# A hybrid decoder layer on one NeuronCore: the attention's division moved behind its value products, and gate work cut into quarters

## The chip, the cores and the metric

The kernel runs on one core of a Trainium2 chip. The time is device microseconds of one execution of the whole program, inputs and weights read from HBM and the result written back. The kernel before was run three times outside the profiler; one more execution was profiled, and all rows below come from that one.

The engines are named as in the profile: PE is TensorE (PEld its weight loads), DVE is VectorE, ACT is ScalarE, POOL is GpSimd, SP issues nearly all DMAs. "SPq", "DVEq" and so on are the engines' instruction queues.

## What is computed

One decoder layer on x of 1024 tokens by 1024 channels, all in float32: a norm, one input projection, two mixers side by side, an output projection, a second norm and a gated MLP with a short convolution. The change touches the end of mixer A (its gated norm) and mixer B (the attention):

```python
z = z_a.astype(jnp.float32).reshape(B, S, GDN_HEADS, GDN_HEAD_DIM)
o_a = (rmsnorm(o_a, gdn_norm_w) * jax.nn.silu(z)).reshape(B, S, GDN_WIDTH).astype(x.dtype)
...
s = jnp.where(valid, s, -jnp.inf)
m = jnp.max(s, axis=-1)
p = jnp.exp(s - m[..., None])
den = jnp.sum(p, axis=-1)
num = jnp.einsum('...nqk,...nkd->...nqd', p, vv)
...
out = num_tot / den_tot[..., None]
...
x = x + jnp.concatenate([o_a, o_b], axis=-1) @ w_out
```

Mixer B has eight heads of 64 channels and three patterns of keys (near, every fourth, every sixteenth). The kernel joins the three patterns into one softmax per query, with the logarithm of each key's multiplicity in a mask.

## The kernel before

**Layout.** Activations lie transposed, channels on the 128 partitions and tokens along the free axis. Each float32 matrix product is three products of 128x128 by 128x512, of a high and a low part of each factor (`mm3`, L245). The low part is a subtraction on VectorE, the high part a rounding copy on ScalarE (`split`, L251).

**An order written out by a planner.** `Weave` (L46) runs several generators ("streams") with levels, keeps an estimate of TensorE's time and of when each tile is ready, and lets the most urgent stream that is ready emit its next products. The matmuls carry a token (`TOKEN`), so TensorE executes them in exactly this order and stands still if an operand is late. Instructions of the other engines are put in order by a scheduler with priorities; those written through `uv` and `ua` (L157, L158) go ahead of others. Work that can wait is cut into *pieces*: `defer` (L199) stores them, `background` (L226) emits one when the planner thinks VectorE is free, `flush` (L204) emits what must be there now. While attention or the recurrence runs (`chains` isn't empty), each piece is tied between the urgent operations around it.

**The streams around the change.** `dense` (L577) multiplies the normed input with 25 columns of 128 weights; the list `DENSE` (L42) ends with the attention's columns `("a", pair, part)` and the four `z` columns. Each column is two halves of 24 products. Its products fill TensorE while attention waits for the softmax. A column's weights come through the tag `wst` with two buffers.

`attention` (L1035) goes through four pairs of heads (`pi`), each in two halves of the queries (`hh`), so eight *groups*; a group has four query blocks `n`, handled in two pairs of blocks. Per pair `advance` (L1169) turns the probabilities of the pair before on TensorE (`turn`, L1112), makes the scores of this pair (`scores`, L1046), and multiplies the turned probabilities of the pair before with the values (`values`, L1131; after a group's last pair also `merge_classes`, L1140, for the far keys). `normalise` (L1078) is the softmax: minimum and mask on VectorE, exponential with its sum on ScalarE, then a reciprocal and two scalings on VectorE, in the tile `sm`. `turn` waits in the plan for `sm` of the pair's first block. A group's output lies in one PSUM bank `po` of the tag "ch" (two banks); `give` (L1154) copies it to `oT` in a reordered layout, and SP stores it in `mixer`.

`finish` (L984) sums the squares of mixer A's output and sends the sums through DRAM (`sdram`, `ft`) to POOL, which makes the norm's factor; `fdram` holds it. In `dense`, each z column loads the head's output `og` and the factor spread over all partitions, `fB` (`to_all`, L690), and POOL multiplies them (L636). `gate` (L552) makes tanh on ScalarE and two products on VectorE of 128x1024 each, `zz` and `og`; for the first three z columns it is put off behind a softmax (`put_off`). `scaled` (L507) evicts a z half from PSUM in one instruction.

After the dense columns, `mixer_splits` (L1217) splits the eight mixer tiles, `out_proj` (L1245) multiplies them with the output weights, first for two output blocks at once (j = 0 in banks "hf", j = 1 in banks "ch", the latter once attention is done), then block by block.

## Time and profile before

| What | Value |
|---|---|
| median of three runs | 1187.69 us (1185.7 to 1190.31) |
| the profiled execution's own time | 1187.61 us |
| its span in the profile | 1185.0 us, mean granted TensorE clock 0.998 |
| recurrence and dense columns, chains on | up to about 300 us |
| attention woven with dense columns | about 300 to 460 us |
| output projection | about 455 to 545 us |
| MLP | about 545 to 1185 us |

How to read the rows: in the timeline a row is the start in us, the duration in us (of all of a merged run), engine, line, operation, out<-in with partitions x elements, the count, and in brackets the idle time of that engine just before it with what ended it. L142, L144, L233 and L242 are lines of helpers through which nearly all instructions go: L142 plain, L144 urgent, L233 matmul, L242 half transposes of the probabilities. In group rows the numbers behind the bar are busy us of the whole group and mean ns of one; then idle time before them. Matmuls overlap: a 128x512 product's record is 0.39 us long while one starts every 0.23 us.

### The profile page before, as it was taken

How to read it: one execution, taken by the hardware profiler on the slowest of the kernel's cores; microseconds unless marked ns; L12 is line 12 of the kernel's file. 1: busy time of each engine (PE TensorE's matmuls, PEld its weight loads, DVE VectorE, ACT ScalarE, POOL GpSimd, SP SyncE). 2: the span in 40 equal slices, each digit the busy share in tenths (PEclk: the TensorE clock that was granted, in tenths of full speed). 3: DMA queues.
4: the chain of work that ended last, by engine and by line, in shares of the span. 5: the costliest groups of instructions: out<-in, count | busy, mean ns of one | idle time of the engine just before them, and what ended most of it. 6: DMA issues, size and time to landing. Idle time of an engine off the chain costs nothing.

```text
span 1185.0 us, 18118 instructions
## 1 busy us (share of the span) xinstructions
PE 1173.8 (99%) x6962; PEld 969.6 (82%) x6962; DVE 968.7 (82%) x1556; ACT 555.4 (47%) x996; POOL 65.8 (6%) x50
## 2 busy tenths in 40 slices
PE   9999999999999999999999999999999999999997
PEld 7888888898777778888888888888888888888887
DVE  7786997464687876768999898988889889998987
ACT  7483333333344444655554444544444543546452
POOL 0312001003130000000000000000000000000001
PEclk9999999999999999999999999999999999999999
DMA  7424566838563314443231313222231395456624
GB/s 240 108 88 138 149 162 181 263 103 250 192 187 100 87 51 150 164 139 107 89 107 54 107 54 107 72 88 93 68 107 54 132 386 184 127 177 223 239 96 160
DMA packets 120310, 165.34 MB, mean 140 GB/s; under 512 B 55008, under 2 KB 70176, under 8 KB 120224
## 3 DMA queue, kind: packets, MB, share of 16 engines
q1 hardware_dynamic: 119504, 163.66, 43.2%
q8 instruction: 54, 0.88, 0.3%
q10 hardware_dynamic: 720, 0.53, 0.1%
q14 instruction: 32, 0.26, 0.1%
HBM read 123.99 MB, written 40.17 MB: 139 GB/s over the span
## 4 chain that ended last, share of the span: by engine, by line
PE 96%; DVE 2%; SPq 1%; ACT 1%; DMA 0%; issue 0%; DVEq 0%; ACTq 0%
PE ps L233 46%; PE pa L233 20%; PE dw L233 18%; PE pc L233 10%; PE ps L242 1%; SPq L142 1%; DVE sm L144 1%; PE ps L237 1%; PE warm L233 0%; DMA wst<-in_wi 0%; DVE wlo L142 0%; DVE x1h L142 0%; ACT sm L144 0%; PE pd L233 0%; DVE pt L144 0%
## 5 line engine op out<-in xcount | busy, mean ns | idle before, releaser
L233 PE MATMUL dw<-pr 128*128 128x512 f32 (+1 forms) x984 | 211.4, 376 | 0.0
L233 PEld LDWEIGHTS dw<-pr 128*128 128x128 f32 x984 | 176.7, 188 | 33.6
L233 PE MATMUL ps<-xhi,whi 128*128 128x512 f32 x448 | 183.3, 409 | 0.0
L233 PE MATMUL ps<-xhi,wlo 128*128 128x512 f32 x448 | 175.2, 391 | 0.0
L233 PE MATMUL ps<-xlo,whi 128*128 128x512 f32 x448 | 175.0, 391 | 0.0
L233 PE MATMUL pa<-T,pair 128*128 128x512 f32 x528 | 126.8, 389 | 0.0
L233 PEld LDWEIGHTS pa<-T,pair 128*128 128x128 f32 x528 | 99.1, 188 | 20.6
L233 PEld LDWEIGHTS ps<-xhi,whi 128*128 128x128 f32 x448 | 84.5, 189 | 19.5 <-issue 3.1
L233 PEld LDWEIGHTS ps<-xhi,wlo 128*128 128x128 f32 x448 | 84.2, 188 | 18.4
L233 PEld LDWEIGHTS ps<-xlo,whi 128*128 128x128 f32 x448 | 84.6, 189 | 14.7
L142 ACT ACTIVATE u<-pa 128x512 f32<-128x512 f32 x44 | 26.4, 599 | 114.3 <-PE pa L233 114.3
L142 DVE SCALAR_TENSOR_TENSOR y<-xu,fcw,y 128x1023 f32<-128x1023 f32 (+1 forms) x44 | 56.3, 1281 | 22.1 <-ACT y L142 22.0
L142 ACT ACTIVATE pr<-wd 128x1024 fp32r<-128x1024 f32 x33 | 35.0, 1060 | 72.3 <-DVE wd L142 35.4
L142 DVE TENSOR_TENSOR wlo<-wst,whi 128x256 fp32r<-128x256 f32 (+3 forms) x65 | 50.9, 802 | 15.6 <-ACT whi L142 15.6
L233 PE MATMUL pa<-B,A 128*128 128x512 f32 x264 | 63.5, 389 | 0.0
L233 PE MATMUL pc<-T,S 128*128 128x512 f32 x264 | 63.4, 389 | 0.0
L233 PE MATMUL pc<-B,pair 128*128 128x512 f32 x264 | 63.4, 389 | 0.0
L233 PE MATMUL pa<-T,S 128*128 128x512 f32 x264 | 63.4, 389 | 0.0
L142 DVE TENSOR_TENSOR wst<-wst 128x512 f32<-128x512 f32 x88 | 60.4, 686 | 0.8
L233 PE MATMUL ps<-B,pair 128*128 128x512 f32 x252 | 60.5, 389 | 0.0
L144 ACT ACTIVATE sm<-sm,mx 128x128 f32<-128x128 f32 (+7 forms) x64 | 35.4, 555 | 51.6 <-DVE mx L144 51.6
L142 ACT ACTIVATE whi<-wst 128x1024 fp32r<-128x1024 f32 (+2 forms) x38 | 38.4, 1011 | 42.2 <-PE ps L233 28.4
(243 smaller groups left out, 2199.4 us busy)
## 6 DMA issues: line engine op xcount, KB each, us to landing
wst<-in_wu SPq DMA_DIRECT2D x44, 512.0 KB, 3.6
wd<-in_wd SPq DMA_DIRECT2D x44, 512.0 KB, 4.4
wst<-in_wi SPq DMA_DIRECT2D x25, 512.0 KB, 4.4
upark<-y SPq DMA_DIRECT2D x22, 512.0 KB, 3.4
r<-upark SPq DMA_DIRECT2D x22, 512.0 KB, 10.1
wa<-in_wd SPq DMA_DIRECT2D x22, 256.0 KB, 3.0
apark<-aqkv SPq DMA_DIRECT2D x8, 512.0 KB, 4.8
wst<-in_wo SPq DMA_DIRECT2D x8, 512.0 KB, 3.7
```

The source lines that it names most:

```text
L142: return getattr(eng, op)(*a, **kw)
L144: inst = getattr(eng, op)(*a, **kw)
L233: tc.stamp_issue_order_token(nc.tensor.matmul(dst, lhs, rhs, start=start, stop=stop, **kw).ins, TOKEN)
L237: tc.stamp_issue_order_token(nc.tensor.transpose(dst, src, ident).ins, TOKEN)
L242: tc.stamp_issue_order_token(nc.tensor.transpose(dst, src[rows], ident[rows, rows]).ins, TOKEN)
```

## The change

- The softmax's reciprocal and scaling of `sm` go; the probabilities stay undivided through turn, values and far keys.
- The sums go to a constant tile `dens` (eight columns for a group). After a group's last softmax `spread` takes the reciprocal of all eight columns, turns them (32x32 blocks) on VectorE, writes four pieces to DRAM (`dendram`) and loads them back so that each of the 64 partitions of a head holds the reciprocals of the 512 queries, in `rB`, a tile of the tag "uy" (five slots, of which four were in use in attention).
- `give` multiplies `po` with `rB`, in four instructions of 128x128, instead of copying. They wait in a list `lazy` until the load was emitted and no other piece is due; a list `soon` holds the spread's steps.
- `turn` waits in the plan for both blocks' `sm`, with other slacks (-0.1, -0.6 instead of -1.0 for the first block alone).
- The factor's product moves from POOL to VectorE, in quarters of 256 columns, and from the z columns to `finish`; a z column waits for ("g", h).
- z's eviction and the two gate products are issued in quarters through the piece list, tanh in halves; the `put_off` list goes.
- The first output weights are prepared while the last dense column runs, their subtractions in quarters; so are those of the third block. j = 1 starts once the last output is given. `background` runs on until all lists are empty.
- `sd` is SP's queue with another cost in the plan (0.4 + 0.0003 per element, 2.2 until landing); the loads of `vc` are booked by it as well.

```diff
@@ constants and lists
+    sd = Engine(wv, nc.sync, "sync", 0.4, 0.0003, 2.2)
-    pieces, chains, seen = [], set(), {}
+    pieces, lazy, soon, chains, seen = [], [], [], set(), {}
...
     def background():
-        while "attention" not in wv.done:
-            if pieces and wv.free.get("vector", 0.0) <= wv.pe + 0.05 and wv.need(*pieces[0][2]) <= 0.0:
-                one_piece()
+        while not {"attention", "firsts"} <= wv.done or pieces or lazy or soon:
+            while soon and wv.need(*soon[0][2]) <= 0.0:
+                one_piece(soon)
+            for queue in (pieces, lazy):
+                if (queue and wv.free.get("vector", 0.0) <= wv.pe + 0.05 and wv.need(*queue[0][2]) <= 0.0
+                        and all("spread" in g for g in queue[0][3:])):
+                    one_piece(queue)
+                    break
             yield 0.3
+        chains.discard("attention")
+        wv.done.add("drained")
...
+    dendram = dp.tile([2 * H, 8, P], F32, name="dendram")
+    dens = const("dens", [P, 4, 32])
+    ve.memset(dens, 1.0)
@@ gate
+    quarters = [slice(256 * i, 256 * i + 256) for i in range(4)]
+    def gate(og, xr, pt):
...
+            turned_on(slice(0, 512))
+            turned_on(slice(512, 1024))
+        defer(*[(y, lambda c=c: ve.scalar_tensor_tensor(y[:, c], y[:, c], 1.0, xr[:, c], op0=OP.add, op1=OP.mult), [y])
+                for c in quarters])
+        defer(*[(og, lambda c=c: product(c), [y, og]) for c in quarters])
@@ dense
             if kind == "z":
                 yield from wv.until(("o", h))
+                yield from wv.until(("g", h))
...
-            if i + 1 < len(DENSE):
+            if i + 1 == len(DENSE):
+                first_out.append(wk(I["wo"][MORDER[0]], None, 4))
+            else:
                 nxt = wk(None, raw.pop(), 4 if chains else 1)
...
+                if kind == "z":
+                    for c in quarters[2 * hh:2 * hh + 2]:
+                        defer((pt, lambda c=c, pt=pt, xr=xr: ve.tensor_tensor(xr[:, c], pt[:, c.start % 512:c.start % 512 + 256],
+                                                                              rstdB[:, c], op=OP.mult), [pt]))
...
-                to_all(fB[0], fdram[h])
-                po_.tensor_tensor(og, og, fB[0], op=OP.mult)
...
+                gate(gated[h], xr, pt)
@@ finish, behind "f"
+        fB = A("fB", "go")
+        for h in range(H):
+            og = gated[h] = A("og", "kT*")
+            sy.dma_start(og, mixer[h])
+            to_all(fB, fdram[h])
+            while wv.need(og, fB) > 0.0:
+                yield wv.need(og, fB)
+            defer(*[(og, lambda c=c, og=og: ve.tensor_tensor(og[:, c], og[:, c], fB[:, c], op=OP.mult),
+                     [og, fB]) for c in quarters])
+            while any(t is og for t, *_ in pieces):
+                yield 0.3
+            wv.done.add(("g", h))
@@ attention
-            uv.reciprocal(den, den)
-            for e in range(2):
-                div = uv.tensor_scalar(sm[:, e, :wd], sm[:, e, :wd], den[:, e:e + 1], None, op0=OP.mult)
+        def spread(g):
+            i = 2 * g["pi"] + g["hh"]
+            if not g["hh"]:
+                rBs.append(A("rB", "uy"))
+            rB = g["rB"] = rBs[-1][:, half(g["hh"])]
+            row, held = dens[:, 2 + i % 2], dendram[i]
+            def turn_():
+                ve.reciprocal(g["den"][:, :8], g["den"][:, :8])
+                inst = ve.transpose(row, g["den"])
+                for b in range(4):
+                    sd.dma_start(held[:, 32 * b:32 * b + 32], row[32 * b:32 * b + 8])
+                return inst
+            def load():
+                for e in range(2):
+                    r = held[4 * e:4 * e + 4]
+                    sd.dma_start(rB[64 * e:64 * e + 64],
+                                  bass.AP(tensor=r.tensor, offset=r.offset, ap=[[0, 64], [1, 4 * P]]))
+                g["spread"] = True
+            soon.append((g["po"], turn_, [g["den"]]))
+            soon.append((g["po"], load, [dendram]))
...
-                return max(wv.need(pair[0]["sm"]) + TSLACK[0], *[wv.slot_free(t, n) for t in ("asc", "atr")
+                return max(wv.need(pair[0]["sm"]) + (-0.1), wv.need(pair[1]["sm"]) + (-0.6), *[wv.slot_free(t, n) for t in ("asc", "atr")
...
-            ve.tensor_copy(oT.rearrange("p (n u c) -> p n c u", n=4, c=4),
-                           po.rearrange("p (n c u) -> p n c u", n=4, c=4))
+            def part_(n):
+                inst = ve.tensor_tensor(oT.rearrange("p (n u c) -> p n c u", n=4, c=4)[:, n],
+                                        po.rearrange("p (n c u) -> p n c u", n=4, c=4)[:, n],
+                                        g["rB"][:, n * P:n * P + P].rearrange("p (c u) -> p c u", c=4), op=OP.mult)
...
+            lazy.extend((po, lambda n=n: part_(n), [po, g["rB"]], g) for n in range(4))
...
+                if len(groups) > 1:
+                    flush(groups[-2], soon)
+                    flush(groups[-2], lazy)
                 po = bank("ch")
@@ out_proj
-        ws = [wk(I["wo"][m]) for m in MORDER[:2]]
+        made = first_out + [wk(I["wo"][MORDER[1]], None, 4)]
...
-            now = [a for a in todo if ("ot", a[0]) in wv.done and (a[1] == 0 or "attention" in wv.done)]
+            now = [a for a in todo if ("ot", a[0]) in wv.done and (a[1] == 0 or ("o", 7) in wv.done)]
```

101 lines of the change are left out of this document (53 added, 48 removed).

## The prediction

> **What bounds the kernel now.** I read the page first: span, busy shares, chain of waits.
>
> ```profile
> span 1185.0 us, 18118 instructions
> PE 1173.8 (99%) x6962; PEld 969.6 (82%) x6962; DVE 968.7 (82%) x1556; ACT 555.4 (47%) x996; POOL 65.8 (6%) x50
> ...
> PE 96%; DVE 2%; SPq 1%; ACT 1%; DMA 0%; issue 0%; DVEq 0%; ACTq 0%
> ```
>
> TensorE is the bound. The change adds and removes no matmul: the new turn of the reciprocals runs on VectorE, everything else is VectorE, ScalarE, POOL or DMA work. So it can pay only where TensorE stands still or changes its kind of work, and only in the stage it touches, attention woven with the dense columns, which the second view gives as one window (busy us of each engine, instructions in brackets).
>
> ```profile
> 300.00:460.00 160.00, 157.02 (x1723) 119.59 (x1722) 126.91 (x363) 67.62 (x208) 18.53 (x13) 1.00 0.40 120
> ```
>
> TensorE lacks 160 - 157.0 = 3.0 us there; VectorE is busy 79%. What follows is dense, from the chain of waits in order of time:
>
> ```profile
> 457.80 85.54 PE ps L233 x376
> ```
>
> That is 85.54/376 = 0.2275 us a product, with no gap to win. Third view: TensorE in order of time at every place of the stage where a bracket reports idle time.
>
> ```profile
> 335.64 0.71 PE L242 MATMUL ps<-ident,sm 64*128 64x64 f32 x16 [1.44 <-DVE sm L144]
> 336.55 0.73 PE L242 MATMUL ps<-ident,sm 64*128 64x64 f32 x16 [0.20 <-DVE sm L144]
> ...
> 397.45 2.39 PE L233 MATMUL ps<-kT,qT 64*128 64x256 f32 x40 [0.59 <-ACT pb L144]
> ...
> 405.57 0.50 PE L233 MATMUL ps<-xhi,whi 128*128 128x512 f32 x1
> ...
> 407.85 1.26 PE L233 MATMUL ps<-kT,qT 64*128 64x128 f32 x8
> ...
> 412.31 0.60 PE L242 MATMUL ps<-ident,sm 64*128 64x64 f32 x8 [0.57 <-DVE sm L144]
> ```
>
> The four brackets add to 1.44 + 0.20 + 0.59 + 0.57 = **2.80 us**. Three (2.21 us) wait for `sm`, the scaled softmax, the very tensor whose scaling goes. As ends of matmuls are modelled, some waiting hides inside long records; comparing runs of like products I put that at about 2 us more, an estimate. So about **5 us** is all that can be recovered as waiting, 0.4% of 1187.6.
>
> Why the largest wait was so long is seen on VectorE and POOL in order of time:
>
> ```profile
> 326.43 3.51 DVE L142 TENSOR_TENSOR wlo<-wst,whi 128x256 fp32r<-128x256 f32 x4
> ...
> 333.06 2.77 DVE L144 TENSOR_SCALAR sm<-sm,mx 128x416 f32<-128x416 f32 x2
> ...
> 401.92 0.78 DVE L144 TENSOR_SCALAR sm<-sm,mx 128x416 f32<-128x416 f32 x2
> ```
> ```profile
> 326.28 2.38 POOL L142 TENSOR_TENSOR og<-og,fB 128x1024 f32<-128x1024 f32 x1 [5.28 <-DMA fB<-fdram]
> ...
> 332.88 2.37 POOL L142 TENSOR_TENSOR og<-og,fB 128x1024 f32<-128x1024 f32 x1 [3.75 <-DMA fB<-fdram]
> ```
>
> The same two scalings take 0.78 us alone and 2.77 us while POOL multiplies `og`: 1.99 us lost, more than the 1.64 us for which TensorE then stood. The four subtractions beside the first POOL product took 3.51 us too; three alone take 1.08 (a row further down).
>
> **The change part by part.** VectorE's groups in the stage, with their shapes (busy us, mean ns):
>
> ```profile
> L142 DVE TENSOR_TENSOR wlo<-wst,whi 128x256 fp32r<-128x256 f32 x25 | 11.5, 499 | 0.0
> L142 DVE TENSOR_TENSOR aqkv<-ps,rstdB 128x256 f32<-128x256 f32 x16 | 9.1, 625 | 0.5 <-PE ps L233 0.5
> L142 DVE COPY oT<-ps 128x512 f32<-128x512 f32 x8 | 8.5, 1059 | 0.0
> L142 DVE TENSOR_TENSOR xr<-ps,rstdB 128x512 f32<-128x512 f32 x8 | 5.5, 689 | 1.5 <-PE ps L233 1.4
> L144 DVE RECIPROCAL mx<-mx 128x2 f32<-128x2 f32 x32 | 5.2, 164 | 3.1 <-ACT sm L144 2.5
> L142 DVE SCALAR_TENSOR_TENSOR og<-og,gw,zz 128x1024 f32<-128x1024 f32 x4 | 5.1, 1281 | 0.1
> L142 DVE SCALAR_TENSOR_TENSOR zz<-zz,xr 128x1024 f32<-128x1024 f32 x4 | 4.9, 1224 | 1.1 <-ACT zz L142 1.1
> L142 DVE STREAM_TRANSPOSE avt<-aqkv 128x256 f32<-128x256 f32 x8 | 3.0, 416 | 0.0
> L144 DVE COPY pt<-ps 128x128 f32<-128x128 f32 x8 | 1.9, 276 | 2.7 <-PE ps L242 2.7
> ```
> ```profile
> L144 DVE TENSOR_SCALAR sm<-sm,mx 128x128 f32<-128x128 f32 (+7 forms) x64 | 24.9, 431 | 1.2
> ```
>
> *Removed from VectorE*: the scalings 24.9, their reciprocals 5.2, the copies of `oT` 8.5, and, to be re-issued in quarters, z's evictions 5.5, `zz` 4.9, `og` 5.1: 54.1 us. *Added*: 32 multiplications of 128x128 out of PSUM, between the 0.28 us of a 128x128 copy and half a reordered 128x256 eviction and more (at most 0.63); I take 0.30, as half of 0.63 is 0.31: 9.6 us. Eight reciprocals of eight columns and eight turns of 128x32, each about 0.2 (the 0.16 of two columns below, the 0.42 of eight times the turn above): 3.2. Quarters for z, factor, sigmoid and gate, 16 each, at 0.42 (between 0.36, a third of 1.08 in the row quoted further down, and the group's 0.50): 64 x 0.42 = 26.9. Sum 39.7, so VectorE is relieved of 14 us; with the upper ends (20.2 + 6.7 + 32.0 = 58.9) it would gain 5 us of work. The low ends (9.0 + 2.6 + 23.0 = 34.6) give 20 us of relief. This is off TensorE's path except at the waits; I give it no value of its own.
>
> *The wait at 335.64* (1.64 us): turning then needs only the exponentials, no scaling, and POOL's product is gone from beside it: **-1.6**. *At 412.31* (0.57) the same: **-0.6**. *At 397.45* the wait is for `pb`, ScalarE's copy behind VectorE's `pt`, which stood behind a whole z eviction; a quarter is shorter by 0.69 - 0.42 = 0.27 us: **-0.3** of the 0.59. *Of the hidden 2 us* I take half, **-1.0**: the same chains feed them, but not all of it can be told from the cost of changing products. *Against it* **+0.5**: the added quarters must find their place between the urgent operations, and any one of them just ahead of a `pt` copy costs up to 0.42 us. Sum -1.6 - 0.6 - 0.3 - 1.0 + 0.5 = **-3.0 us**.
>
> *Spreading the reciprocals* is the new wait: four writes to DRAM, then two loads that wait for them, all on SP's queue, 48 issues in eight groups. The nearest row is the norm factor's own trip, written in four pieces and loaded back:
>
> ```profile
> 306.70 2.80 SPq L142 DMA_DIRECT2D sdram<-sums  x4
> ...
> 313.75 0.33 SPq L142 DMA_DIRECT2D ft<-sdram  x1
> ```
> ```profile
> 315.56 5.44 POOL L142 TENSOR_TENSOR ft<-ft,mhalf 128x32 f32<-128x32 f32 x1 [21.75 <-DMA ft<-sdram]
> ```
>
> 315.56 - 306.70 = 8.9 us. The kernel's planner, by the constants of the diff, books 4 x 0.41 + 2.2 + 2 x 0.55 + 2.2 = 7.1 us. The answer must be there before the output bank is due again, two groups on; the groups follow each other every (447.23 - 322.72)/7 = 17.8 us:
>
> ```profile
> 322.72 1.06 DVE L142 COPY oT<-ps 128x512 f32<-128x512 f32 x1
> ...
> 447.23 1.07 DVE L142 COPY oT<-ps 128x512 f32<-128x512 f32 x1
> ```
>
> So I cost it at nothing, covered by at least one group's matmuls. Without that cover a multiplication waits on VectorE for the load, and all urgent softmax work is queued behind it (rival below). The Trainium skill, "DMA: Bandwidth & Descriptors", section "Anatomy of one DMA — SWDGE (gpsimd) path", gives a fixed cost of about 2.0 us for a DMA, most of it the write receipt. Two in a row would make 4 us and the issues, well inside 7.1; the row's 8.9 us speaks for more, and I go by the row. Its specifications also put the least transfer at full rate at 512 bytes, which the 128-byte rows written here miss; no row shows what that costs.
>
> *The end of attention.* The last `oT` copy above ends at 448.3, and the first output product starts at 455.41:
>
> ```profile
> 455.41 0.39 PE L233 MATMUL ps<-ohi,whi 128*128 128x512 f32 x1
> ```
> ```profile
> 386.45 0.69 DVE L142 TENSOR_TENSOR xr<-ps,rstdB 128x512 f32<-128x512 f32 x1
> ...
> 439.04 0.17 DVE L144 RECIPROCAL mx<-mx 128x2 f32<-128x2 f32 x1 [0.30 <-ACT sm L144]
> ```
>
> The last reciprocal of now, which follows the last exponential, starts at 439.04, so 439.0 + 0.4 + 8.9 + 4 x 0.30 = 449.5, 1.2 us later than now, still 5.9 us before 455.41: hidden. The output weights' subtractions move earlier, in quarters, under the same dense products; `dens` costs one memset at the start. The factor's product moves from the z columns to right after `f`; its loads of `og` and `fB` keep their order on SP, the first two factors were there at 326.28 and 332.88 (above), four by that pace before 350, and z's first eviction comes at 386.45, so z need not wait for it. The other account for `vc` and the new slacks in `turn` change only the plan.
>
> **Rivals.** *One, slower: the reciprocals come late.* For three of the eight groups SP is then issuing the next heads' keys and values:
>
> ```profile
> 393.29 5.07 SPq L142 DMA_DIRECT2D vc<-avdram  x8
> ...
> 399.10 0.36 SPq L142 DMA_DIRECT2D wst<-in_wi  x1
> ```
> ```profile
> 388.66 1.08 DVE L142 TENSOR_TENSOR wlo<-wst,whi 128x256 fp32r<-128x256 f32 x3
> ```
>
> Eight issues hold the queue for 5.07 us, and a weight load behind them leaves only at 399.10. A spread behind these arrives after 8.9 + 5.1 = 14 us where 7.1 were booked in the worst case; VectorE in order then stands up to 6.9 us, of which a dense run (405.57 to 407.85, 2.28 us) covers about 2.3: 4.6 us on TensorE, three times 13.8; in the five other groups 8.9 - 7.1 = 1.8 us is covered. Two of the three in full and one by half make +11.5; less the 3.0: **1196.1**. It decides once the loads land over 2.3 us after the place where the planner put the multiplications. For it: SP is in order and its queue is full there. Against: the diff books `vc` dearer (0.55 an issue), and multiplications go out only when nothing else is waiting.
>
> *Two, no change:* VectorE was not the bound, the waits reappear at other points of a fixed TensorE order (`pb`, the quarters). Savings of 3.5 against new waits of 3.5: **1187.6**. For it: the bracket at 397.45 is not one of scaling.
>
> *Three, more:* every wait goes (-4.8), and the shorter softmax lets some of the changes between dense and attention products fall together. The nine dense products from 405.57 to 407.85 take 2.28 instead of 9 x 0.2275 = 2.05 us, so a change costs 0.23; eight fewer of some thirty: -1.8. **1181.0**. Against: the banks of scores still have to come free.
>
> **How the numbers follow.** The profiled execution took 1187.6 us (span 1185.0), as good as the median of 1187.69, so 1187.6 - 3.0 = **1184.6**. Chances: forecast 0.43, rival one 0.24, two 0.20, three 0.13. About 0.5%, or 5.9 us, is what a measurement of this kernel can tell from no change: below 1181.8 lies rival three, above 1193.6 rival one, hence faster 0.13, same 0.63, slower 0.24. The forecast's own range is 1182.5 to 1186.5 (savings of 5 us and 1 us); half of each outer rival is left out: 1181 to 1196, which also holds the unknown costs of the quarters.
>
> **What would show it.** Right: no `TENSOR_SCALAR` on `sm`, no POOL product of `og`, no bracket over 0.5 us on the turning matmuls; VectorE busy in this stage lower by 10 to 15 us. Wrong: a multiplication of `oT` whose idle time before it ends with the DMA of `rB`; matmuls waiting for `ps` behind it; weights (`whi`) waiting for `wst` behind the spread on SP. The out projection should start without a new gap. If TensorE's lack in this stage doesn't fall from 3.0 us, the reasoning fails.

## The result, and the profile after

| | before | after |
|---|---|---|
| median (9 runs each, same chip) | 1187.69 us (1185.7 to 1190.85) | **1184.32 us** (1183.52 to 1185.22) |
| ratio | 1 | 0.9971 (95%: 0.996 to 0.9983) |
| profiled execution, span in it | 1187.61, 1185.0 us | 1184.53, 1182.5 us |
| mean granted TensorE clock | 0.998 | 0.998 |

The changed kernel is 0.29% faster, 0.3 us from the forecast of 1184.6. With nine runs a side, the interval separates even this from no change, though the prediction took 0.5% as the least that can be told. The small net hides two larger movements, and the forecast had both wrong in size.

From the page of the changed kernel, the engines with busy time and share:

```profile
PE 1172.2 (99%) x6962; PEld 967.8 (82%) x6962; DVE 949.1 (80%) x1558; ACT 555.3 (47%) x1000; POOL 54.6 (5%) x46
```

TensorE's matmuls are the same 6962. VectorE has lost 968.7 - 949.1 = 19.6 us, the span only 2.5. Next the windows (length, then busy us of PE, PEld, DVE, ACT and POOL with instructions, granted clock, DMA share, GB/s): first of the kernel before, where its largest wait lay, then of the changed kernel for the same stretch and for the whole stage.

```profile
325.00:350.00 25.00, 23.36 (x274) 17.82 (x270) 23.29 (x65) 10.24 (x37) 10.79 (x7) 1.00 0.63 178
```
```profile
325.00:350.00 25.00, 24.95 (x275) 18.96 (x276) 16.16 (x59) 9.82 (x35) 0.84 (x2) 1.00 0.74 209
...
300.00:460.00 160.00, 158.08 (x1734) 120.49 (x1734) 107.65 (x365) 71.23 (x218) 9.00 (x9) 1.00 0.45 137
```

In the 25 us that held the wait at 335.64, VectorE drops from 23.3 to 16.2 us and POOL from 10.8 to 0.8, and TensorE stands for 0.05 instead of 1.64 us. Over 160 us TensorE still lacks 1.92 us. That it isn't the old lack is seen in its timeline (start, duration, operation, idle time before it in brackets):

```profile
447.32 1.51 PE L242 MATMUL ps<-pb,vc 128*64 128x128 f32 x32
448.76 0.50 PE L242 MATMUL ps<-xhi,whi 128*128 128x512 f32 x1
...
450.93 0.39 PE L242 MATMUL ps<-ohi,whi 128*128 128x512 f32 x1
...
452.04 0.47 PE L242 MATMUL ps<-ohi,whi 128*128 128x512 f32 x1 [0.26 <-DVE xr L142]
...
458.26 0.50 PE L242 MATMUL ps<-ohi,whi 128*128 128x512 f32 x1 [1.51 <-DVE oT L142]
```

The matmul helpers have the lines L242 and L251 here, L233 and L242 before. No attention matmul waits any more; the only two brackets of these 160 us lie behind attention, in the output projection. So I use two lengths for every kernel: the **stage**, from the start of the products that sum the squares of mixer A's output (`osq,picks`) to the first output product (`ohi,whi`), and the **tail**, from there to the end of the span. The opening rows, first of the kernel before and then of the changed one:

```profile
302.52 1.93 PE L233 MATMUL ps<-osq,picks 128*32 128x256 f32 x32
```
```profile
302.70 1.93 PE L242 MATMUL ps<-osq,picks 128*32 128x256 f32 x32
```

Before, the stage is 455.41 - 302.52 = 152.89 us and the tail 1185.0 - 455.41 = 729.59. After, the stage is 450.93 - 302.70 = 148.23 and the tail 731.57. **The stage gained 4.66 us and the tail gave back 1.98.** The two brackets make 1.77 us of the 1.98. From the first scores of attention to the first output product, TensorE's timeline has 369 dense products in either kernel.

Why the tail waits: attention's last matmuls (`pb,vc`) are followed by 9 dense products in the changed kernel (448.76 to 450.93), but by 42 in the kernel before, whose timeline has these two rows:

```profile
444.31 1.51 PE L233 MATMUL ps<-pb,vc 128*64 128x128 f32 x32
445.75 0.50 PE L233 MATMUL ps<-xhi,whi 128*128 128x512 f32 x1
```

(455.41 - 445.75)/0.2275 = 42. Those dense products were fillers that attention had not used, and they covered the last eviction. The changed kernel spends them inside the stage, where they pay, and comes to the output projection with little left to hide behind; the last matmuls of its attention even start 3.0 us later (447.32 against 444.31). The timelines of VectorE, ScalarE and SP in the changed kernel show what is then late:

```profile
442.11 0.19 DVE L142 RECIPROCAL dens<-dens 128x8 f32<-128x8 f32 x1
...
445.50 0.20 DVE L142 STREAM_TRANSPOSE dens<-dens 128x32 f32<-128x32 f32 x1
445.63 1.39 DVE L142 TENSOR_TENSOR wlo<-wst,whi 128x256 fp32r<-128x256 f32 x4
...
453.51 0.76 DVE L142 SCALAR_TENSOR_TENSOR zz<-zz,xr 128x256 f32<-128x256 f32 x2 [0.95 <-ACT zz L142]
454.19 1.67 DVE L142 SCALAR_TENSOR_TENSOR og<-og,gw,zz 128x256 f32<-128x256 f32 x4
455.77 1.43 DVE L142 TENSOR_TENSOR wlo<-wst,whi 128x256 fp32r<-128x256 f32 x4
457.12 1.09 DVE L142 TENSOR_TENSOR oT<-ps,rB 128x128 f32<-128x128 f32 x4
```
```profile
450.95 2.01 ACT L142 ACTIVATE whi<-wst 128x1024 fp32r<-128x1024 f32 x2 [2.55 <-DMA wst<-in_wo]
```
```profile
445.73 1.30 SPq L142 DMA_DIRECT2D dendram<-dens  x4
447.13 0.36 SPq L142 DMA_DIRECT2D wst<-in_wo  x1
```

The last group's reciprocal and its turn come behind pieces of the gate, a split of a mixer tile and urgent copies, so the four writes leave only at 445.73. The multiplication of `oT` then stands behind z's gate and a subtraction of output weights and ends at 458.21, where TensorE goes on with j = 1, whose bank it frees.

The gate itself is late for a reason further back. A load of output weights leaves SP at 447.13, just after the subtraction that began at 445.63 has ended (447.02) and freed a buffer. ScalarE stands 2.55 us for this load before two roundings, z's last tanh comes behind them, and VectorE's gate waits 0.95 us for that tanh. The output weights' subtractions also come later than in the kernel before, whose VectorE timeline has the first two at

```profile
441.89 1.22 DVE L142 TENSOR_TENSOR wlo<-wst,whi 128x1024 fp32r<-128x1024 f32 x1
...
448.13 1.22 DVE L142 TENSOR_TENSOR wlo<-wst,whi 128x1024 fp32r<-128x1024 f32 x1
```

where the changed kernel has them at 445.63 and not before 455.77.

### The profile page after: what moved, and what is told of

It reads as the page before. It is cut to its first block, busy times and chain, and to the rows that moved or that the text cites. A ratio compares the mean times of both kernels' runs of the same rounds, so it can differ in the third digit from the quotient of the medians.

```text
span 1182.5 us, 18166 instructions
## 1 busy us (share of the span) xinstructions
PE 1172.2 (99%) x6962; PEld 967.8 (82%) x6962; DVE 949.1 (80%) x1558; ACT 555.3 (47%) x1000; POOL 54.6 (5%) x46
## 4 chain that ended last, share of the span: by engine, by line
PE 95%; DVE 3%; DMA 1%; ACT 1%; issue 0%; SPq 0%; DVEq 0%; ACTq 0%
PE ps L242 45%; PE pa L242 20%; PE dw L242 18%; PE pc L242 10%; PE ps L251 1%; DVE kT L142 1%; PE ps L246 1%; PE warm L242 0%; DVE x1h L142 0%; DMA vn<-avdram 0%; DVE xr L142 0%; SPq L142 0%; DMA wst<-in_wo 0%; PE pd L242 0%; DVE pt L144 0%
## 5 line engine op out<-in xcount | busy, mean ns | idle before, releaser
L242 PE MATMUL dw<-pr 128*128 128x512 f32 (+1 forms) x984 | 211.4, 376 | 0.0
L242 PEld LDWEIGHTS dw<-pr 128*128 128x128 f32 x984 | 176.7, 188 | 33.6
L242 PE MATMUL ps<-xhi,whi 128*128 128x512 f32 x448 | 183.3, 409 | 0.0
L242 PE MATMUL ps<-xhi,wlo 128*128 128x512 f32 x448 | 175.0, 391 | 0.0
L242 PE MATMUL ps<-xlo,whi 128*128 128x512 f32 x448 | 174.9, 390 | 0.0
L242 PE MATMUL pa<-T,pair 128*128 128x512 f32 x528 | 126.8, 389 | 0.0
L242 PEld LDWEIGHTS pa<-T,pair 128*128 128x128 f32 x528 | 99.1, 188 | 20.6
L242 PEld LDWEIGHTS ps<-xhi,whi 128*128 128x128 f32 x448 | 84.3, 188 | 19.6 <-issue 3.3
L242 PEld LDWEIGHTS ps<-xhi,wlo 128*128 128x128 f32 x448 | 84.2, 188 | 18.4
L242 PEld LDWEIGHTS ps<-xlo,whi 128*128 128x128 f32 x448 | 84.5, 189 | 14.7
L242 PE MATMUL pa<-B,A 128*128 128x512 f32 x264 | 63.5, 389 | 0.0
L242 PE MATMUL pc<-T,S 128*128 128x512 f32 x264 | 63.4, 389 | 0.0
L242 PE MATMUL pc<-B,pair 128*128 128x512 f32 x264 | 63.4, 389 | 0.0
L242 PE MATMUL pa<-T,S 128*128 128x512 f32 x264 | 63.4, 389 | 0.0
L242 PE MATMUL ps<-B,pair 128*128 128x512 f32 x252 | 60.5, 389 | 0.0
L242 PEld LDWEIGHTS pc<-B,pair 128*128 128x128 f32 x264 | 49.6, 188 | 10.3
```

What stands on the lines that cost most here:

```text
L242: tc.stamp_issue_order_token(nc.tensor.matmul(dst, lhs, rhs, start=start, stop=stop, **kw).ins, TOKEN)
```

## The experiments

A row of the table is one kernel: its median, the ratio to the kernel before on the same chip, then the stage and tail of its profiled execution. The kernel before was run again beside each batch of them, with medians of 1187.61 to 1188.13 us; "slower by" is against that median. That one execution was the slowest of its kernel for "last group urgent" (1190.53 us), 2.2 us above the median for "old slack" (1192.21), and the fastest for "no quarters" (1184.73), "slacks alone" (1204.74) and "factor on VectorE alone" (1199.29), so these stages and tails stand for the medians only roughly.

| kernel | median us | ratio (95%) | stage | tail |
|---|---|---|---|---|
| before | 1187.69 | 1 | 152.89 | 729.59 |
| after | 1184.32 | 0.9971 (0.996 to 0.9983) | 148.23 | 731.57 |
| factor on VectorE alone | 1201.67 | 1.0114 (1.0099 to 1.013) | 165.97 | 729.73 |
| slacks alone | 1206.57 | 1.0159 (1.0145 to 1.0173) | - | - |
| no division | 1184.88 | 0.9975 (0.9964 to 0.9985) | 150.60 | 729.70 |
| factor back on POOL | 1195.56 | 1.0063 (1.0051 to 1.0076) | 152.05 | 738.00 |
| last group urgent | 1188.72 | 1.0013 (1.0004 to 1.0022) | 148.28 | 737.05 |
| last group divided | 1187.75 | 1.0004 (0.9995 to 1.0013) | 152.91 | 730.12 |
| no quarters | 1186.25 | 0.9991 (0.9982 to 1.0) | 148.13 | 732.72 |
| old slack | 1190.01 | 1.0032 (1.002 to 1.0045) | 151.09 | 735.68 |
| lows free | 1183.25 | 0.9961 (0.9947 to 0.9975) | 148.13 | 731.22 |
| lows and output free | 1184.25 | 0.9967 (0.9954 to 0.9979) | 148.10 | 732.00 |
| no factor | 1185.76 | 0.9983 (0.9974 to 0.9992) | 151.13 | 729.61 |
| no spread | 1187.90 | 1.0002 (0.9993 to 1.0011) | 148.13 | 735.05 |

In two kernels, "no division" and "old slack", the first turning goes ahead of the product that opens the stage, and TensorE waits 0.76 us for its copy there. The row of the first:

```profile
303.77 1.93 PE L233 MATMUL ps<-osq,picks 128*32 128x256 f32 x32 [0.76 <-DVE pt L144]
```

The first scores lie 4.47 us ahead of this product in the two (303.77 - 299.30 in the first) and 3.80 us in the others (302.52 - 298.72 in the kernel before), so 0.67 us are added to their stages (149.93 and 150.42 as measured) to make them comparable.

Six kernels have a stage of 148.1 to 148.3 us. None of them has a bracket in it, so this looks like TensorE's work there without a wait.

### One part alone, on the kernel before

**The factor's product on VectorE, whole, where it stood:**

```diff
-                po_.tensor_tensor(og, og, fB[0], op=OP.mult)
+                ve.tensor_tensor(og, og, fB[0], op=OP.mult)
```

> The kernel before, with one edit: the factor's product (og by fB) is on VectorE, in one instruction, instead of on POOL. Theory (POOL's product slows the scalings beside it, and the wait at 335.64 comes from that): the two scalings that took 2.77 us take 0.8 us, the wait of 1.64 us there goes; VectorE carries 4 x 1.2 us more; 1.0 to 1.6 us faster than before. Rival (the gain of the change comes from the division alone): no faster than before, perhaps 0.5 us slower.

Measured: 1201.67 us, slower by 13.5. VectorE's timeline has the product four times, the first of them here, and TensorE's what follows from it:

```profile
324.96 1.23 DVE L142 TENSOR_TENSOR og<-og,fB 128x1024 f32<-128x1024 f32 x1 [4.72 <-DMA fB<-fdram]
```
```profile
328.54 1.74 PE L242 MATMUL ps<-ident,sm 64*128 64x64 f32 x24 [4.72 <-DVE sm L144]
...
331.24 0.63 PE L233 MATMUL ps<-xhi,wlo 128*128 128x512 f32 x1
331.66 0.63 PE L233 MATMUL ps<-xhi,whi 128*128 128x512 f32 x1
```

The product stands on VectorE at a place where `fB` has not landed (4.72, 0.15, 1.25 and 2.18 us, 8.3 us in all), and the softmax behind it waits with it. On POOL this waiting had been free. Both expectations missed this. The last two rows are read in the section on the hardware. So the price isn't the 1.23 us of the product but the DMA ahead of it; the change pays nothing for it because it takes the product out of the columns and issues it only when the plan has `fB` landed: none of its quarters has a bracket in VectorE's timeline there.

**The turn's slacks alone:**

```diff
-                return max(wv.need(pair[0]["sm"]) + TSLACK[0], *[wv.slot_free(t, n) for t in ("asc", "atr")
+                return max(wv.need(pair[0]["sm"]) + (-0.1), wv.need(pair[1]["sm"]) + (-0.6), *[wv.slot_free(t, n) for t in ("asc", "atr")
```

> The kernel before, with one edit: turn waits in the plan for both blocks' softmax with the slacks of the change (-0.1 and -0.6). Theory (the gain comes from less work ahead of the turning): the waits on the scaling shrink partly because more dense products stand before them, at most 1.5 us faster, and the scalings next to POOL's product still take 2.8 us. Rival (the plan's slacks are the gain, the division is beside the point): 2.5 to 3.5 us faster, as the whole change.

Measured: 1206.57 us, slower by 18.4, the dearest of all. With the softmax still long, the planner puts dense runs of up to 27 products ahead of a turning, and the dense columns run out at 431.7 us while attention goes on to 482.6. From there TensorE stands bare at its turnings, by up to 4.25 us (its timeline, and the window):

```profile
476.00 1.11 PE L242 MATMUL ps<-ident,sm 64*128 64x64 f32 x16 [4.25 <-DVE sm L144]
```
```profile
440.00:490.00 50.00, 38.22 (x390) 29.26 (x389) 26.63 (x74) 17.12 (x51) 0.00 (x0) 0.86 0.16 50
```

11.8 us are missing in these 50. A stage and a tail can't be told apart here, since output products already fill in while attention runs. The slack sets how fast the fillers are spent.

**No division**, which leaves out the reciprocals and the scalings and puts nothing in their place, so the attention's output stays undivided:

```diff
...
-            uv.reciprocal(den, den)
-            for e in range(2):
-                div = uv.tensor_scalar(sm[:, e, :wd], sm[:, e, :wd], den[:, e:e + 1], None, op0=OP.mult)
-            return exp, div
+            return exp, least
```

> The kernel before without the softmax's reciprocals and scalings; nothing takes their place, so the attention's outputs stay undivided. Theory: all waits that end with sm go (2.2 us by the brackets, and part of the hidden waiting), 2.2 to 3.5 us faster, POOL's product no longer holding anything up. Rival (POOL's product stalls VectorE's subtractions and evictions just as well, so the division matters little): under 1.5 us faster.

Measured: 1184.88 us; the stage is shorter by 152.89 - 150.60 = 2.29 us and the tail unchanged (729.70). This is the worth of taking the scalings out with the old slack and without what the change puts in their place. The four brackets of before are gone, the one at 335.64 with them, although POOL is as busy as before (10.89 us in the window from 325 to 350, in which TensorE is busy throughout):

```profile
325.00:350.00 25.00, 25.00 (x317) 19.19 (x317) 17.85 (x55) 11.39 (x41) 10.89 (x7) 1.00 0.44 120
```

New ones of 0.76, 0.39, 0.20 and 0.20 us stand near its start, at 303.77 to 318.04, where the turnings now come sooner than the copies and exponentials.

**No factor**, which leaves out the product of `og` and `fB` on every engine:

```diff
-                po_.tensor_tensor(og, og, fB[0], op=OP.mult)
```

> The kernel before with the factor's product left out on every engine (og isn't multiplied by fB). Theory (POOL's product beside the scalings made the wait at 335.64): that wait goes, 0.8 to 1.6 us faster than before, the wait at 412.31 stays. Rival (without POOL's product the scalings are still late): within 0.4 us of before.

Measured: 1185.76 us, the stage shorter by 1.76 us. VectorE's timeline has the two groups of before that ran beside POOL's products:

```profile
326.57 1.42 DVE L142 TENSOR_TENSOR wlo<-wst,whi 128x256 fp32r<-128x256 f32 x4
...
331.74 0.78 DVE L144 TENSOR_SCALAR sm<-sm,mx 128x416 f32<-128x416 f32 x2
```

They took 3.51 and 2.77 us before. With the POOL product gone both are at their price alone, and the wait at 335.64 is gone while the scalings are still there. The two parts may not be added: each of them alone removes this same wait. With the scalings gone, POOL's product at its old place costs TensorE no wait in that stretch (25.00 us busy of 25 in the kernel without division).

### One part undone, in the changed kernel

**The factor back on POOL**, at its new place in `finish`:

```diff
-            defer(*[(og, lambda c=c, og=og: ve.tensor_tensor(og[:, c], og[:, c], fB[:, c], op=OP.mult),
-                     [og, fB]) for c in quarters])
-            while any(t is og for t, *_ in pieces):
-                yield 0.3
+            po_.tensor_tensor(og, og, fB, op=OP.mult)
```

> The changed kernel, with the factor's product put back on POOL in one instruction per head. Theory: with no scalings in SBUF left to hold up, POOL's product costs little: within 0.5 us of the changed kernel, 2.5 to 3.5 us faster than before; VectorE carries 16 quarters less. Rival (sharing with POOL was the main loss): 1.5 us or more slower than the changed kernel, with a wait of TensorE beside a POOL product.

Measured: 1195.56 us, 11 us above the changed kernel. Here late reciprocals, the prediction's rival one, are seen at work, in the timelines of SP, POOL, VectorE and TensorE:

```profile
343.39 0.32 SPq L142 DMA_DIRECT2D fB<-fdram  x1
...
344.71 2.53 SPq L142 DMA_DIRECT2D dendram<-dens  x4
350.04 1.09 SPq L142 DMA_DIRECT2D rB<-dendram  x2
```
```profile
340.97 2.40 POOL L142 TENSOR_TENSOR og<-og,fB 128x1024 f32<-128x1024 f32 x1 [4.41 <-DMA fB<-fdram]
```
```profile
342.00 1.65 DVE L142 TENSOR_TENSOR wlo<-wst,whi 128x256 fp32r<-128x256 f32 x1
...
353.83 1.06 DVE L142 TENSOR_TENSOR oT<-ps,rB 128x128 f32<-128x128 f32 x4 [7.38 <-issue]
```
```profile
355.38 0.50 PE L242 MATMUL ps<-xhi,whi 128*128 128x512 f32 x1 [3.65 <-DVE dens L142]
355.72 0.39 PE L242 MATMUL ps<-xlo,whi 128*128 128x512 f32 x1
```

The bracket of the multiplication names no tile, but `rB` is the one operand that is still on its way: its loads leave at 350.04. VectorE stands 7.38 us, near the 6.9 of the rival's worst case, and TensorE 3.65. The reason is not the one the rival gave, the loads of `vc` ahead on SP: these leave at 353.20, behind the spread's. The reciprocals are turned at 335.31, but on SP's queue their writes stand behind the load of the next factor, which leaves only when POOL's product has ended and freed `fB` (340.97 + 2.40 = 343.37), and behind a store of `aqkv`, whose eviction ends at 344.16, behind a subtraction that took 1.65 us beside the same product. So they leave 9.4 us after the turn. The tail loses 6.4 us more against the changed kernel. So the spread was free in the changed kernel by its place in the plan and on SP's queue, not by nature.

**The last group urgent**: its reciprocal, turn and DMAs at once behind its last softmax, its multiplications ahead of other pieces:

```diff
+                v = uv if final else ve
+                v.reciprocal(g["den"][:, :8], g["den"][:, :8])
+                inst = v.transpose(row, g["den"])
...
+            if final:
+                turn_()
+                load()
...
-                inst = ve.tensor_tensor(oT.rearrange("p (n u c) -> p n c u", n=4, c=4)[:, n],
+                inst = (uv if final else ve).tensor_tensor(oT.rearrange("p (n u c) -> p n c u", n=4, c=4)[:, n],
```

> The changed kernel, with the last group's steps made urgent: its reciprocals, their turn and the DMAs are written right after its last softmax, and the four multiplications of its output go out as urgent operations once the group's products are done. Theory (the wait of 1.51 us at 458.26 is the last output standing behind z's gate on VectorE): the first multiplications start near 453 instead of 457.1, the bracket goes, 1.0 to 1.5 us faster than the changed kernel. Rival (the output is late because the reciprocals are): VectorE waits for rB at that place, and the gate of z behind it is late: not faster.

Measured: 1188.72 us, 4.4 above the changed kernel. In the timelines of VectorE, SP, ScalarE and TensorE:

```profile
447.05 1.41 DVE L142 TENSOR_TENSOR wlo<-wst,whi 128x256 fp32r<-128x256 f32 x4
```
```profile
448.50 0.36 SPq L142 DMA_DIRECT2D wst<-in_wo  x1
```
```profile
453.58 2.01 ACT L142 ACTIVATE whi<-wst 128x1024 fp32r<-128x1024 f32 x2 [3.72 <-DMA wst<-in_wo]
```
```profile
458.87 0.79 PE L242 MATMUL ps<-ohi,wlo 128*128 128x512 f32 x1 [2.50 <-DVE wlo L142]
```

The multiplication, at 452.24, is 4.9 us earlier, as meant. But the subtraction that frees the weights' buffer starts at 447.05 instead of 445.63, so the load leaves at 448.50 instead of 447.13 (SP waited for this subtraction and not for the spread; 0.67 us of the 1.4 are this execution's later start). ScalarE stands 3.72 us for it, and TensorE's wait returns as one for `xr` (1.53 us), for `whi` (0.68) and then for `wlo` (2.50).

**The last group divided** as before, without a spread:

```diff
-            if pair[1]["u"] == 3:
+            if pair[1]["u"] == 3 and not (pair[0]["g"]["pi"] == 3 and pair[0]["g"]["hh"] == 1):
...
+            if last_group:
+                uv.reciprocal(den, den)
+                for e in range(2):
+                    uv.tensor_scalar(sm[:, e, :wd], sm[:, e, :wd], den[:, e:e + 1], None, op0=OP.mult)
...
+                ve.tensor_copy(oT.rearrange("p (n u c) -> p n c u", n=4, c=4),
+                               po.rearrange("p (n c u) -> p n c u", n=4, c=4))
```

> The changed kernel, with the last group alone divided as before (reciprocals and scalings in sm, output copied), so that its output needs no spread. Theory: no wait at the output projection's start for oT (1.5 us less), but the scalings of two pairs come back before the turning: 0.5 to 1.5 us faster than the changed kernel. Rival (the tail is set by z's gate and the weights): same time as the changed kernel.

Measured: 1187.75 us, no gain. The tail improves to 730.12, but the stage is back at 152.91: in the plan its last turnings wait for scalings again, 27 dense products go ahead of the last one instead of 15, and attention's last products stand without fillers:

```profile
452.42 2.83 PE L242 MATMUL ps<-pb,vc 128*64 128x128 f32 x32 [2.31 <-ACT pb L144]
```

**No quarters**: z's eviction in halves, the factor's and the gate's products whole, still through the piece list:

```diff
-    quarters = [slice(256 * i, 256 * i + 256) for i in range(4)]
+    quarters = [slice(0, 1024)]
+    zparts = [slice(512 * i, 512 * i + 512) for i in range(2)]
...
-                    for c in quarters[2 * hh:2 * hh + 2]:
+                    for c in zparts[hh:hh + 1]:
```

> The changed kernel, with z's evictions in halves of 512 and zz, og and the factor's product in one instruction each instead of quarters (weights stay in quarters). Theory (a long piece ahead of an urgent copy is what cost 0.59 us at 397.45): waits of 0.3 to 1.0 us come back at one to three of the turnings, 0.5 to 2 us slower than the changed kernel. Rival (quarters only add fixed cost on VectorE): same or up to 0.5 us faster.

Measured: 1186.25 us, 1.9 us above the changed kernel; the two intervals just touch, so the difference is likely and not more. The stage is 148.13 us and has no bracket, the tail is 1.15 us longer in its profiled execution, with two waits for `oT` (1.39 and 1.32 us). So it is slower by about what was expected, but not by waits at the turnings: the cut into quarters is not what shortens the stage, and what it may be worth lies in the tail.

**The old slack** in the changed kernel:

```diff
-                return max(wv.need(pair[0]["sm"]) + (-0.1), wv.need(pair[1]["sm"]) + (-0.6), *[wv.slot_free(t, n) for t in ("asc", "atr")
+                return max(wv.need(pair[0]["sm"]) + TSLACK[0], *[wv.slot_free(t, n) for t in ("asc", "atr")
```

> The changed kernel, with turn's old condition (the first block's softmax alone, 1.0 us early). Theory (less work ahead of the turning is the gain, slacks only move dense products): 9 instead of 12 dense products before the turnings, some 30 left over for the end, the wait of 1.51 us there goes, but TensorE waits 0.2 to 0.5 us for exponentials at several turnings: within 2 us of the changed kernel. Rival (the slacks are half of the gain): 2 to 4 us slower than the changed kernel.

Measured: 1190.01 us, 5.7 above the changed kernel and more than either expectation. The stage is longer by 2.86 us, 1.16 of it in brackets (0.76, 0.20 and 0.20). Now 63 dense products are left behind attention, and the tail is worse all the same, by 4.1 us. TensorE's timeline and windows there:

```profile
455.87 0.47 PE L242 MATMUL ps<-ohi,whi 128*128 128x512 f32 x1 [1.42 <-DVE xr L142]
...
459.84 0.79 PE L242 MATMUL ps<-ohi,wlo 128*128 128x512 f32 x1 [2.59 <-DVE wlo L142]
460.43 0.63 PE L242 MATMUL ps<-ohi,whi 128*128 128x512 f32 x1
460.86 0.63 PE L242 MATMUL ps<-olo,whi 128*128 128x512 f32 x1
```
```profile
455.00:460.00 5.00, 1.54 (x6) 1.02 (x6) 4.97 (x16) 1.69 (x2) 0.00 (x0) 0.78 0.57 185
460.00:465.00 5.00, 5.00 (x13) 3.93 (x14) 5.00 (x12) 2.53 (x4) 0.00 (x0) 0.54 0.88 286
```

So left-over fillers alone don't cover the tail: VectorE is busy for 4.97 of the 5 us in which TensorE waits for the weights' subtraction, which stands behind z's gate there. The left-over products are those of the last z columns, whose gate can follow only behind them. What binds is VectorE's order at the end.

### The tail

**Lows free**: the subtractions of the second output weights outside the list of pieces, so that the scheduler may place them:

```diff
-        made = first_out + [wk(I["wo"][MORDER[1]], None, 4)]
+        made = first_out + [wk(I["wo"][MORDER[1]])]
```

> The changed kernel, with the second output weights' subtraction in one instruction outside the piece list, so that it isn't tied behind z's gate. Theory (the wait of 1.51 us at 458.26 is made by the order of the pieces on VectorE: gate, weights, output): the subtraction moves ahead of the gate, the wait shrinks to 0.5 to 1.2 us, 0.3 to 1 us faster than the changed kernel. Rival (the last output's multiplication alone holds it): unchanged.

Measured: 1183.25 us, the fastest median of all, but its interval overlaps that of the change, so it isn't shown to beat it. TensorE's timeline:

```profile
457.11 0.50 PE L242 MATMUL ps<-ohi,whi 128*128 128x512 f32 x1 [1.47 <-DVE oT L142]
```

The multiplication is 1.15 us earlier (455.97), of which 0.65 us are this execution's earlier start, and TensorE's products ahead of it are earlier too: the bracket stays.

**Lows and output free**: the last group's multiplications outside the chain of pieces too:

```diff
-                return inst
+                return None if g["pi"] == 3 and hh == 1 else inst
```

> As the run with the second output weights' subtraction outside the piece list, and the last group's multiplications outside it too. Theory: both stand ahead of z's gate, as soon as rB has landed (near 453), the bracket of 1.51 us goes: 1 to 1.5 us faster than the changed kernel, about 1183. Rival (the spread's landing sets it): VectorE waits for rB, z's gate is late, and the wait moves to the product of the fourth mixer tile: no gain.

Measured: 1184.25 us. VectorE and TensorE:

```profile
454.88 1.07 DVE L142 TENSOR_TENSOR oT<-ps,rB 128x128 f32<-128x128 f32 x4 [2.85 <-DMA rB<-dendram]
```
```profile
457.06 0.50 PE L242 MATMUL ps<-ohi,wlo 128*128 128x512 f32 x1 [1.41 <-DVE wlo L142]
```

Put ahead of the gate, the multiplication meets the reciprocals before they are there and holds VectorE for 2.85 us; the weights' subtraction is late instead. This also gives the length of a trip whose end nothing but its own loads holds up: its writes leave SP at 445.20, and 454.88 - 445.20 = 9.7 us, with a weight load and a store issued among its DMAs.

**No spread**: the four instructions of the last step copy without `rB`, and no reciprocal travels; the output stays undivided:

```diff
-            if pair[1]["u"] == 3:
-                spread(pair[0]["g"])
...
-                inst = ve.tensor_tensor(oT.rearrange("p (n u c) -> p n c u", n=4, c=4)[:, n],
-                                        po.rearrange("p (n c u) -> p n c u", n=4, c=4)[:, n],
-                                        g["rB"][:, n * P:n * P + P].rearrange("p (c u) -> p c u", c=4), op=OP.mult)
+                inst = ve.tensor_copy(oT.rearrange("p (n u c) -> p n c u", n=4, c=4)[:, n],
+                                      po.rearrange("p (n c u) -> p n c u", n=4, c=4)[:, n])
...
-            lazy.extend((po, lambda n=n: part_(n), [po, g["rB"]], g) for n in range(4))
+            lazy.extend((po, lambda n=n: part_(n), [po]) for n in range(4))
```

> The changed kernel without the spread and without the multiplication: the output is copied in four parts and stays undivided, no DMA for reciprocals. Theory (the spread is hidden everywhere but at the last group): 0.5 to 1.8 us faster than the changed kernel, by the wait at the output projection's start alone. Rival (the spread's DMAs and VectorE's work cost in each group): 2.5 us or more faster.

Measured: 1187.90 us, 3.6 above the changed kernel, where both expectations had it faster. The stage is 148.13 us, 0.10 below the changed kernel's: inside the stage the spreads cost TensorE nothing that could be measured. The tail is 3.5 us worse without them. TensorE waits there 0.26 us for `xr`, 0.55 for `whi` and then for the subtraction:

```profile
457.62 0.71 PE L242 MATMUL ps<-ohi,wlo 128*128 128x512 f32 x1 [2.94 <-DVE wlo L142]
```

The copies of the output stand at 456.69, ahead of the subtraction at 457.13. So the wait of 1.51 us is not the price of the spread's trip: with no trip at all the tail is longer. No kernel got rid of the tail's loss without a loss elsewhere. Each edit that moved one of VectorE's last steps made another late. Their common source, the weights' load that waits for a subtraction and has z's tanh behind it on ScalarE, wasn't moved by itself, so what order would hide all of this is left open.

## Why the prediction was right, and where it wasn't

**What bounds the kernel, and what can be recovered: right.** About 5 us of waiting was the bound given, 4.66 came. Of this 2.80 us were in brackets, and 1.86 showed in none.

**The gain in the stage: under-sized, because a term was put at nothing.** The forecast had -3.0 us and gave the new slacks no value ("change only the plan"). The runs split the 4.66 us in this way: the scalings taken out, -2.29; the rest of the change but the slacks, +0.49 (150.60 to 151.09); the slacks, -2.86 (151.09 to 148.23). So the slacks are the largest single part, and taking the division out comes next. The price of -1.6 for the wait at 335.64 was right in size: POOL's product taken away alone gave -1.76. But the same wait also goes with the scalings alone, so once they are gone the factor's move takes no wait out of that stretch any more. The 0.59 us at 397.45 went whole, and without quarters too, so a shorter eviction is not what removed it. The +0.5 us for quarters among urgent operations was not there: with and without them the stage is 148.1 to 148.2 us. Where the 1.86 us sat is not shown.

**Spreading the reciprocals: right by its cover, inside the stage.** The trip was 9.7 us where it could be seen best, 0.8 above the nearest row's 8.9 and 2.6 above what the planner books. The Trainium skill, "DMA: Bandwidth & Descriptors", section "Anatomy of one DMA — SWDGE (gpsimd) path", gives a fixed cost of about 2.0 us for a DMA issued by GpSimd. Two of these make an estimate of 4 us, less than half of the 9.7; SP issues the DMAs here, and the row was the better guide. The first seven groups cost TensorE nothing. VectorE meets one late load, of the first group, and TensorE has no bracket from it:

```profile
332.03 1.10 DVE L142 TENSOR_TENSOR oT<-ps,rB 128x128 f32<-128x128 f32 x4 [0.94 <-DMA rB<-dendram]
```

**The end of attention: this step failed.** It called the last spread hidden by 449.5 against 455.41, and put the output weights' subtractions earlier than before. Instead the multiplication ended at 458.21, TensorE waited 1.51 us for it, and the tail lost 1.98. Four things were wrong. The start was: the step let the spread leave at 439.4, right behind the last exponential of before, but that exponential ends at 440.68 in the changed kernel, the reciprocal and the turn are pieces behind other work, and the writes leave at 445.73. The end was: the multiplication was priced by its own duration and not by what the planner puts ahead of it, z's gate and output weights. The subtractions were: they came 3.7 us and at least 7.6 us later, and the weights' next load and z's tanh with them. And 455.41 was held fixed, though the same sum shortened the stage: the first output product comes 4.5 us earlier in time, and the fillers behind attention shrink from 42 products (9.6 us) to 9 (2.0 us). What hides an operation before a change need not be there after it. The trip itself isn't to blame for all of this: without any spread the tail was longer still.

**"The other account for vc and the new slacks change only the plan", and the factor's move at nothing: too cheap an answer.** In this combination the stage shows no loss. But the slacks alone cost 18.4 us, and are worth 5.7 inside the change, half of it in the stage; the product on VectorE without its move costs 13.5, and the move without VectorE 11. The account for `vc` wasn't tried by itself. For a kernel whose order is planned, a changed plan is a term of the sum.

**VectorE's relief: higher than forecast.** The window went from 126.91 to 107.65 us, 19.3 instead of 14, near the upper bound of 20, and over the whole span it is 19.6. Part of this is that the 32 multiplications took 8.7 us against 9.6 estimated, and part that POOL no longer holds VectorE up: without POOL's product alone the same window falls from 126.91 to 123.36 us, 3.6 us that the sum didn't have.

**The rivals.** One (late reciprocals) didn't happen in this kernel, but is real, for another reason, with the factor's product on POOL. Two (no change) fell: the waits did not reappear within the stage. Three (every wait goes) was the truth of the stage as to its waits, 4.66 of 4.8; its further 1.8 us for fewer changes of work are not there: TensorE's timelines have 59 changes between dense and other products before and 61 after.

So the net came out as forecast by luck: a gain forecast 1.7 us too small met a loss of 2.0 us that was left out. The mechanism, waits that end with the softmax, was right. -4.66 + 1.98, and 0.18 for a stage that began later, is the span's -2.5 us; another 0.6 us of the profiled time lies outside the span (1187.61 - 1185.0 before, 1184.53 - 1182.5 after).

## What to carry to other kernels

Count every term of a change, a planner's constants too. Before calling an operation hidden, ask whether its cover is still there after the change: work that fills in is a budget, and a stage that gets shorter takes it from the next. In an in-order kernel the price of a moved instruction is less its duration than what it waits for at its new place and who stands behind it, so a DMA-fed operation belongs where its data have surely landed. Test the parts of a combined change one by one: here two of them alone cost 13 and 18 us, and together with the rest they pay.

## What the runs showed of the hardware

**After a stall the matmuls run slower for a while.** In the kernel with the old slack two waits of 1.42 and 2.59 us fall close together. The granted clock of the next 5 us is 0.54, and products that otherwise start every 0.23 us start every 0.43 (460.43, 460.86). The stall of 4.72 us in the kernel with the factor on VectorE was followed by the same (331.24, 331.66). The wait of 1.51 us in the changed kernel left the products behind it 0.23 us apart. A single wait of 2.31 us, in the kernel with the last group divided, was followed by slow products: the granted clock was 0.50 from 453 to 455, and 32 products of attention took 2.83 us (452.42) where the changed kernel takes 1.51 (447.32). But a single wait of 3.65 us, in the kernel with the factor on POOL, was followed by products 0.23 us apart (355.72 after 355.38 at 0.34, then 0.23). So the price of a stall depends on what surrounds it, and no length at which it sets in can be read from these runs. The Trainium skill, "TensorE: Matmul & The Clock Gate", section "Part 1: The HAM clock gate", states a half rate after an idle window of about 3.4 us that runs free of the program. The half rate agrees (0.43 against 0.23 us). That one wait of 2.31 us was enough, and one of 3.65 us was not, fits a window only if its phase counts and it need not be idle throughout, which no run here separates. The slow products are part of a tail's loss: without spread the waits at its start add to 3.75 us, 2.0 more than in the changed kernel, while the tail is 3.5 longer.

**POOL holds VectorE up nearly until it is done.** The pair of scalings took 2.77 us beside POOL's product, which ended 2.19 us after the pair's start (332.88 + 2.37 - 333.06), and 0.78 without it: 2.77 is nearly 2.19 + 0.78. For the four subtractions it is 3.51 against 2.23 + 1.42 (326.28 + 2.38 - 326.43). The Trainium skill, "SBUF — State Buffer", section "SBUF: two separate sides", calls the ports that the two engines share an exclusive lock and not a split of the bandwidth, and the one that comes second fully blocked; the sum is close to that.
